# A hybrid decoder layer on one core: sums of the FFN's hidden tiles spread over K blocks, a pool opened with waits per tile, the last products reordered

## The chip, the cores and the metric

The kernel runs on one core of a Trainium2 chip. The metric is the device time of one execution, in microseconds (us); lower is better. In this text PE is the matrix engine (TensorE), PEld its weight load, DVE the vector engine, ACT the scalar engine, POOL is GpSimd and SP the engine that issues most loads. ACT issues DMAs as well, and such an issue stands in the same in-order queue as ACT's arithmetic (ACTq in the rows).

## The reference, cut to what matters

One decoder layer on 512 tokens of width 2048, all in fp32: a norm, one input projection, four token mixers side by side, an output projection, then the feed-forward part, and a final norm.

```python
h = rmsnorm(x, norm_ffn_g[l])
x = x + swiglu(h, w_gate[l], w_up[l], w_down[l])   # (silu(h @ w_gate) * (h @ w_up)) @ w_down
...
return rmsnorm(x, norm_final_g)                    # D_FF = 5632, D_MODEL = 2048
```

The change touches the feed-forward part (FFN) and the final norm. Its hidden values, silu(gate) times up, are called h below.

## The kernel before

**Precision.** Every fp32 operand is split into a high part (ACT copies it, rounding to the short fp32r format) and a low part (DVE subtracts the high part from the operand): `split2`, lines 1043 and 1044. A product is three matmuls: high by high, low by high, high by low. So every weight tile costs ACT one copy and DVE one subtraction before PE can use it. `wh`/`wl` are the two halves of a weight step of the gate and up projection, `dh`/`dl` those of the down projection; three buffers hold high parts and four hold low parts, so the high part of step k+2 can't be written before PE has read that of step k-1.

**Seven products.** Gate and up projection, and the down projection, are each done as a 2x2 block product with seven block products (Strassen-Winograd), P1, P5, P6, P3, P7, P4, P2 in that order. Some of them need sums of weight tiles (`T`, formed on DVE, line 1123) and sums of h tiles (S1 to S4, `hs`, DVE).

**The FFN loop.** There are 11 groups `gi` of 512 hidden columns. A group is 28 steps: seven products by four steps `jj`. A step is two K blocks, a K block six matmuls (two token tiles by three). `strassen(k)` calls `w_ahead(k)`, which issues loads for later steps, forms the sum for step k+3 and splits the weights of step k+2; then after each K block it yields, and `run` gives every generator in `side` one hop (`step_side`, line 922). There is no scheduler: each engine works in the order in which the program was written.

**The side work.** After a group's P4 and again after its P2, `got_product` gates the result (`gated`: Silu on ACT, one multiply on DVE, for each of two token tiles) and appends `turn_h`, a generator that waits four hops, then does two halves with a hop between: four PE transposes (`ph`), and `h_sums`, which forms the S tiles, splits those that the down projection will want split, and writes ten tiles per group to DRAM (`ad`) by DMAs issued on ACT (`put`). All of a half's arithmetic and puts are written in one hop. P4's side work (token half 1) runs in P2; P2's (token half 0) runs in P1 of the next group.

**Down projection.** List `ds` holds the products of one K tile each: P1 and P5 alternating, P6 and P3, then P7 followed by P4 with P2's products in between. A product is 12 matmuls. `d_ahead` loads and splits two products ahead. Before the first product the FFN's pool `fp` (`sums`) is closed and the pool `dn` opened over its memory, with tiles for raw weights (`rw`), h tiles (`ar`, split `ah`/`al`), sums `T` and results `c`. In the P7, P4 stage every P7 and P4 forms a sum T on DVE, ACT copies its high part, DVE subtracts; a P2 needs only the two splits.

**Tail.** The last three products (`NT`) are done per token tile t and column half c. `V` holds P2's accumulators (token half 0), `U` those of P4 (token half 1). Squares of finished values go to `ssq`; `finish_tok` takes the square root, the reciprocal, scales four pieces of a token tile and stores them.

Of the kernel before, what the change touches and what calls it, by code (L numbers as in the profile page):

```python
# [39 lines left out]
def hybrid_kernel(ctx, tc, xT, wi, wt, wo, wgu, wdn, vec, rows, sgw, w2a2, g2, pbias, cmask, oneh, addc, fing, out):  # L40
# [14 lines left out]
    def t2(name, shape=(128, 512), dt=F32):  # L55
        return p2.tile(list(shape), dt, name=name, tag="s2")
# [954 lines left out]


    sums = ctx.enter_context(ExitStack())
    fp = sums.enter_context(tc.tile_pool(name="fp", bufs=4))
    xd = dpool.tile([KT, 128, S], F32, name="xd")
    PI = dict(P1=0, P5=1, P6=2, P3=3, P7=4, P4=6, P2=8)
    ad = dpool.tile([10, NG // 4, 128, 2, 256], F32, name="ad")
# [146 lines left out]

    part = {}

    def turn_h(gi, th, h):

        for _ in range(4):
            yield  # L1170
        for b in range(2):
# [5 lines left out]
            h_sums(gi, th, b, p)  # L1177
            yield

    held = {}  # L1180

    def h_sums(gi, th, b, ph):

        def put(p, t, u=0):
            nc.scalar.dma_start(ad[PI[p] + u, gi], t.rearrange("p (b t) -> p b t", b=2))

        def parts(p, src):
            hi, lo = t2("sh", dt=F32R), t2("sl", dt=F32R)
            split2(hi, src, lo)
            put(p, hi.bitcast(F32))  # L1190
            put(p, lo.bitcast(F32), 1)
        if (th, b) == (1, 0):
            held["A21"] = t2("hT")
            ac.activation(held["A21"], ph, AF.Copy)
        elif (th, b) == (1, 1):
            s1 = held["S1"] = t2("hs")
            parts("P4", ph)
            dv.tensor_add(s1, ph, held["A21"])
            put("P5", s1)
        elif (th, b) == (0, 0):  # L1200
            a11, s2 = t2("hT"), t2("hs")
            ac.activation(a11, ph, AF.Copy)
            put("P1", a11)
            dv.tensor_sub(s2, held.pop("S1"), a11)
            held["S2"] = s2
            put("P6", s2)
            s3 = t2("hs")
            dv.tensor_sub(s3, a11, held.pop("A21"))
            parts("P7", s3)
        else:  # L1210
            s4 = t2("hs")
            dv.tensor_sub(s4, ph, held.pop("S2"))
            put("P3", s4)
            parts("P2", ph)

    def got_product(gi, p, t, acc):

        def keep(name):
            part[name, t] = t2(name)
            ac.activation(part[name, t], acc, AF.Copy)  # L1220

        def gated(g, pre, u, i):
            ac.activation(g, pre, AF.Silu, scale=norm2.r[:, i:i + 1])
            dv.scalar_tensor_tensor(g, u, norm2.r[:, i:i + 1], g, op0=OP.mult, op1=OP.mult)
        if p == "P1":
            keep("c11")
        elif p == "P5":
            keep("c22")
        elif p == "P6":
            keep("c12")  # L1230
        elif p == "P3":
            dv.tensor_add(part["c12", t], acc, part["c12", t])
        elif p == "P7":
            dv.tensor_add(part["c22", t], acc, part["c22", t])  # L1234
        elif p == "P4":
            c = part["c21", t] = t2("c21")
            gated(c, acc, part.pop(("c22", t)), 2 + t)
            if t:
                side.append(turn_h(gi, 1, [part.pop(("c21", 0)), part.pop(("c21", 1))]))
        else:  # L1240
            c = part["c11", t]
            dv.tensor_add(c, acc, c)
            gated(c, c, part.pop(("c12", t)), t)
            if t:
                side.append(turn_h(gi, 0, [part.pop(("c11", 0)), part.pop(("c11", 1))]))

    bank = {}

# [57 lines left out]
    n2 = 0  # L1306
    for i, x in enumerate(rest):
        ds.append(x)
        if i % 2 and i > 2 or i == len(rest) - 4:
            ds.append(("P2", n2))  # L1310
            n2 += 1
    assert n2 == NK
# [59 lines left out]
    held.clear()  # L1372
    sums.close()
    mid.close()
    dn = ctx.enter_context(tc.tile_pool(name="dn", bufs=1))
    tags = dict(c=(512, 16), sqd=(512, 1), xq=(1024, 2), T=(1024, NK), ahl=(512, 8), rw=(1024, 5), ar=(512, 4))

    def dt(name, tag, dt=F32):
# [79 lines left out]
    def each():  # L1458
        return [(t, c) for t in range(2) for c in range(2)]
# [8 lines left out]
    def finish_tok(th, t, bank):  # L1468

        q = ssq[:, 2 * th + t]  # L1470
        r = t1("s2", (128, 4))
# [3 lines left out]
        dv.reciprocal(r[:, 3:4], r[:, 2:3])  # L1475
        tok = slice((2 * th + t) * 128, (2 * th + t + 1) * 128)
        for c in range(2):
            o = cf.pop((th, 1, t, c))
            ac.activation(o, o, AF.Copy, scale=r[:, 3:4])
            nc.scalar.dma_start(out[tok, 1024 + c * 512:1536 + c * 512], o)  # L1480
        for c in range(2):
            o = cf.pop((th, 0, t, c))
            dv.scalar_tensor_tensor(o, bank[c] if bank else o, r[:, 3:4], gain[0][:, c * 512:(c + 1) * 512], op0=OP.mult, op1=OP.mult)
            nc.sync.dma_start(out[tok, c * 512:c * 512 + 512], o)

    gain = []
    later = []
    for i in range(2, len(ds) - NT):
        p, kk = ds[i]
        d_ahead(i)  # L1490
        if ds[i] == ("P5", 0):
            V = banks(px)
            xq = load_xq(0, 1)
        elif ds[i] == ("P3", 6):
            turn_x(xq, V)
            xq = load_xq(1, 1)
        elif ds[i] == ("P7", 1):
            V = banks(px)
            turn_x(xq, V, True)
            xq = load_xq(0, 0)  # L1500
            for t, c in each():
                dv.tensor_add(cf[1, 1, t, c], V[t][c], cf[1, 1, t, c])
            V = banks(px)
        elif ds[i] == ("P4", 2):
            turn_x(xq, V)
            xq = load_xq(1, 0)
        elif ds[i] == ("P4", 12):
            turn_x(xq, U)
            del xq
        product(i)  # L1510
        del cutd[i]
        if kk % 2 or i == ends[p]:
            Ac.pop((p, kk // 2), None)
        if i == ends["P1"]:
            for t, c in each():
                cf[0, 0, t, c] = dt("c", "c")
                ac.activation(cf[0, 0, t, c], U[t][c], AF.Copy)
        elif i == ends["P5"]:
            for t, c in each():
                cf[1, 1, t, c] = dt("c", "c")  # L1520
# [22 lines left out]

    tail = range(len(ds) - NT, len(ds))
    d_ahead(len(ds) - NT)
    for th, bank in ((0, V), (1, U)):
        for t in range(2):
            for c in range(2):
                for i in tail:
                    if (ds[i][0] == "P4") == bool(th):  # L1550
                        product(i, [(t, c)])
                o = bank[t][c]
                if th:
                    cf[1, 0, t, c] = dt("c", "c")
                    square(1, 0, t, c, o)
                else:
                    dv.tensor_add(cf[0, 0, t, c], o, cf[0, 0, t, c])
                    square(0, 0, t, c, cf[0, 0, t, c])
            finish_tok(th, t, bank[t] if th else None)


def _constants():
# [81 lines left out]
```

## Time and profile before

| | us |
|---|---|
| median of three runs | 2352.35 (2351.2 to 2355.08) |
| the profiled execution, its own time | 2354.43 |
| its span in the trace | 2352.7 |
| granted PE clock, mean | 0.985 of full |
| mixers and output projection, to | 924 |
| FFN: gate and up projection, from 924 to | 1867 |
| down projection and final norm | to 2352.7 |

The trace is of the profiled execution: times in it run from the span's start. Its own time is 1.7 us more than its span and 2.08 us above the median. Bracketed at the end of a timeline row stands how long the engine was idle before the instruction and what released it.

### The profile page before, as it was taken

To read this page: it belongs to the slowest core of one execution; us is meant where nothing else is said; L and a number is where in the kernel's file an instruction comes from. 1 tells how busy PE (TensorE), PEld (TensorE's weight loads), DVE (VectorE), ACT (ScalarE), POOL (GpSimd) and SP (SyncE) were. 2 spreads that over 40 slices of the span, in tenths; PEclk is the share of its full clock that TensorE was granted. 3 is DMA by queue.
4 is the path that set the end of the run, shared out by engine and by line. 5 is a ranking of instruction groups with operands and counts; after the bars stand their busy time and mean duration, and the time that the engine had idled before them with its cause. 6 is when DMAs were issued, how large, how long until landed. Compare 5 with 4: busy or idle time off the path is not lost.

```text
span 2352.7 us, 29300 instructions
## 1 busy us (share of the span) xinstructions
PE 2245.9 (95%) x11064; PEld 1793.7 (76%) x11064; DVE 1567.0 (67%) x2341; ACT 1013.7 (43%) x1556; POOL 2.3 (0%) x16
## 2 busy tenths in 40 slices
PE   8999999999999997899999999999999879999996
PEld 6788878877777785678777777877877768888785
DVE  6555456654444447877867877777787667777775
ACT  5522222244444435544444444444445344543334
POOL 0000000000000000000000000000000000000000
PEclk9999999999999999999999999999999989999998
DMA  5232323232233235343444455354355187547884
GB/s 185 84 95 73 101 76 92 61 99 82 71 99 108 90 109 178 118 164 121 166 161 152 149 169 180 114 189 166 117 170 192 52 289 250 175 130 241 284 299 177
DMA packets 164541, 342.78 MB, mean 146 GB/s; under 512 B 29296, under 2 KB 34928, under 8 KB 164400
## 3 DMA queue, kind: packets, MB, share of 16 engines
q1 hardware_dynamic: 134832, 290.25, 38.6%
q10 hardware_dynamic: 29568, 50.66, 6.0%
q8 instruction: 87, 1.43, 0.3%
q14 instruction: 54, 0.44, 0.1%
HBM read 302.79 MB, written 38.05 MB: 145 GB/s over the span
## 4 chain that ended last, share of the span: by engine, by line
PE 73%; DVE 13%; ACT 7%; issue 4%; DMA 1%; ACTq 1%; SPq 0%; DVEq 0%
PE prod L1266 8%; PE prod L1267 8%; PE prod L1265 8%; PE acc L144 7%; PE acc L146 7%; PE acc L145 7%; PE bk L1340 4%; PE bk L1341 4%; PE bk L1339 4%; DVE wl L1044 3%; PE acc L162 3%; PE acc L164 2%; PE acc L163 2%; ACT wh L1043 2%; DVE dl L1044 2%
## 5 line engine op out<-in xcount | busy, mean ns | idle before, releaser
L1044 DVE TENSOR_TENSOR wl<-wq,wh 128x512 fp32r<-128x512 f32 x352 | 227.2, 687 | 116.2 <-ACT wh L1043 115.2
L1266 PE MATMUL prod<-wl,h 128*128 128x512 f32 x704 | 282.1, 401 | 22.3 <-DVE wl L1044 22.2
L1265 PE MATMUL prod<-wh,h 128*128 128x512 f32 x704 | 281.5, 400 | 16.4 <-ACT wh L1043 16.4
L1267 PE MATMUL prod<-wh,l 128*128 128x512 f32 x704 | 279.3, 397 | 0.0
L1043 ACT ACTIVATE wh<-wq 128x512 fp32r<-128x512 f32 x352 | 201.4, 623 | 176.0 <-PE prod L1267 105.5
L1339 PE MATMUL bk<-dh,ah 128*128 128x512 f32 x608 | 238.7, 393 | 19.2 <-ACT dh L1043 19.2
L106 DVE TENSOR_TENSOR wlo<-wraw,whi 128x1024 fp32r<-128x1024 f32 x127 | 155.3, 1223 | 140.1 <-ACT whi L105 139.8
L1340 PE MATMUL bk<-dl,ah 128*128 128x512 f32 x608 | 240.0, 395 | 3.7 <-DVE dl L1044 3.7
L1341 PE MATMUL bk<-dh,al 128*128 128x512 f32 x608 | 237.9, 391 | 0.0
L105 ACT ACTIVATE whi<-wraw 128x1024 fp32r<-128x1024 f32 x127 | 134.0, 1055 | 210.7 <-PE acc L145 105.4
L144 PE MATMUL acc<-xhi,whi 128*128 128x512 f32 x512 | 209.3, 409 | 5.6 <-ACT whi L120 5.2
L1043 ACT ACTIVATE wh<-T 128x1024 fp32r<-128x1024 f32 x132 | 139.8, 1059 | 156.9 <-PE prod L1267 111.5
L146 PE MATMUL acc<-xhi,wlo 128*128 128x512 f32 x512 | 200.8, 392 | 1.1 <-DVE wlo L106 1.1
L145 PE MATMUL acc<-xlo,whi 128*128 128x512 f32 x512 | 200.6, 392 | 0.4 <-DVE xlo L235 0.3
L1044 DVE TENSOR_TENSOR wl<-T,wh 128x1024 fp32r<-128x1024 f32 x132 | 161.4, 1223 | 38.3 <-ACT wh L1043 37.7
L1266 PEld LDWEIGHTS prod<-wl,h 128*128 128x128 f32 x704 | 135.3, 192 | 58.9 <-DVE wl L1044 30.9
L1265 PEld LDWEIGHTS prod<-wh,h 128*128 128x128 f32 x704 | 135.1, 192 | 53.7 <-ACT wh L1043 25.5
L1267 PEld LDWEIGHTS prod<-wh,l 128*128 128x128 f32 x704 | 135.2, 192 | 27.7
L1339 PEld LDWEIGHTS bk<-dh,ah 128*128 128x128 f32 x608 | 115.0, 189 | 44.5 <-issue 17.4
L1265 PE MATMUL prod<-wh,hb 128*128 128x512 f32 x352 | 139.7, 397 | 6.7 <-DVE c L1234 6.7
L1043 ACT ACTIVATE dh<-T 128x1024 fp32r<-128x1024 f32 x66 | 70.0, 1061 | 174.1 <-DVE T L1418 57.2
L1340 PEld LDWEIGHTS bk<-dl,ah 128*128 128x128 f32 x608 | 115.0, 189 | 32.3 <-DVE dl L1044 9.2
(316 smaller groups left out, 4159.5 us busy)
## 6 DMA issues: line engine op xcount, KB each, us to landing
wq<-in_wgu_dram SPq DMA_DIRECT2D x440, 256.0 KB, 3.6
rw<-in_wdn_dram SPq DMA_DIRECT2D x134, 512.0 KB, 4.8
wraw<-in_wi_dram SPq DMA_DIRECT2D x63, 512.0 KB, 3.7
wraw<-in_wt_dram SPq DMA_DIRECT2D x32, 512.0 KB, 3.6
wraw<-in_wo_dram SPq DMA_DIRECT2D x32, 512.0 KB, 3.6
ar<-ad SPq DMA_DIRECT2D x44, 256.0 KB, 4.1
ad<-sh ACTq DMA_DIRECT2D x33, 256.0 KB, 3.9
ad<-sl ACTq DMA_DIRECT2D x33, 256.0 KB, 4.1
```

What stands on the lines that cost most here:

```text
L106: dv.tensor_sub(lo, r, hi.bitcast(F32))
L144: pe.matmul(acc[b], wh, xh, start=(c == 0 and k == 0), stop=False)
L145: pe.matmul(acc[b], wh, xl, start=False, stop=False)
L146: pe.matmul(acc[b], wl, xh, start=False, stop=(c == nchunk - 1 and k == 3))
L1043: ac.activation(hi, src, AF.Copy)
L1044: dv.tensor_sub(lo, src, hi.bitcast(F32))
L1265: pe.matmul(acc[t], ah[:, tt], hi[:, u], start=first, stop=False, skip_group_check=more)
L1266: pe.matmul(acc[t], ah[:, tt], lo[:, u], start=False, stop=False, skip_group_check=more)
L1267: pe.matmul(acc[t], al[:, tt], hi[:, u], start=False, stop=(j == 7), skip_group_check=more)
L1339: pe.matmul(o, ah[:, a], hi[:, cc], start=fresh, stop=False, skip_group_check=True)
L1340: pe.matmul(o, ah[:, a], lo[:, cc], start=False, stop=False, skip_group_check=True)
L1341: pe.matmul(o, al[:, a], hi[:, cc], start=False, stop=last, skip_group_check=True)
```

## The change

In the FFN, `turn_h` and `h_sums` become one generator that does one or two operations per hop; the gating moves into it (P4's multiply, and for P2 Silu and multiply); each put is written a hop after what it stores. The pools `fp` and `dn` are opened with `reuse_waits="tile"`. In `ds` P2's products are spread so that the last stands four P4 products before the end. The tail finishes token half 0 earlier, in two pieces, ahead of the last P4 products, and scales and stores with other engines and queues.

```diff
-    fp = sums.enter_context(tc.tile_pool(name="fp", bufs=4))
+    fp = sums.enter_context(tc.tile_pool(name="fp", bufs=4, reuse_waits="tile"))
...
+    def turn_h(gi, th, h, us):
+
+        def put(p, t, u=0):
+            nc.scalar.dma_start(ad[PI[p] + u, gi], t.rearrange("p (b t) -> p b t", b=2))
...
+        rn = [norm2.r[:, 2 * th + t:2 * th + t + 1] for t in range(2)]
+        if th == 0:
+            yield
+            for t in range(2):
+                ac.activation(h[t], h[t], AF.Silu, scale=rn[t])
+        yield
+        for t in range(2):
+            dv.scalar_tensor_tensor(h[t], us[t], rn[t], h[t], op0=OP.mult, op1=OP.mult)
+        us.clear()
+        yield
+        yield
+        p = turned(0)
+        a = t2("hT")
+        ac.activation(a, p, AF.Copy)
+        if th:
...
+            return
+        put("P1", a)
+        yield
+        s2, s3 = t2("hs"), t2("hs")
+        dv.tensor_sub(s3, a, held.pop("A21"))
+        yield
+        hi = high("P7", s3)
+        dv.tensor_sub(s2, held.pop("S1"), a)
+        yield
+        put("P6", s2)
+        lo = low(s3, hi)
+        yield
+        put("P7", lo.bitcast(F32), 1)
+        p = turned(1)
+        hi = high("P2", p)
+        yield
+        s4 = t2("hs")
+        dv.tensor_sub(s4, p, s2)
+        yield
+        put("P3", s4)
+        lo = low(p, hi)
+        yield
+        put("P2", lo.bitcast(F32), 1)
...
-        if i % 2 and i > 2 or i == len(rest) - 4:
+        while n2 < NK and i >= 3 + n2 * 36 // (NK - 1):
             ds.append(("P2", n2))
             n2 += 1
...
-    dn = ctx.enter_context(tc.tile_pool(name="dn", bufs=1))
+    dn = ctx.enter_context(tc.tile_pool(name="dn", bufs=1, reuse_waits="tile"))
...
+        for dh, c in ((1, 0), (0, 0), (0, 1), (1, 1)):
+            o = cf.pop((th, dh, t, c))
+            if dh == 0:
+                dv.scalar_tensor_tensor(o, bank[c] if bank else o, r, gain[0][:, c * 512:(c + 1) * 512], op0=OP.mult, op1=OP.mult)
+            elif c:
+                dv.tensor_scalar(o, o, r, None, op0=OP.mult)
+            else:
+                ac.activation(o, o, AF.Copy, scale=r)
+            col = dh * 1024 + c * 512
+            (nc.sync if dh + c < 2 else nc.scalar).dma_start(out[tok, col:col + 512], o)
...
+        elif p == "P2" and i == ends["P2"]:
+            for t, c in each():
+                dv.tensor_add(cf[0, 0, t, c], V[t][c], cf[0, 0, t, c])
+                square(0, 0, t, c, cf[0, 0, t, c])
+            norm_tok(0, 0)
+            store_tok(0, 0, None)
+        elif p == "P4" and kk == NK - 1 - NT:
+            norm_tok(0, 1)
+            store_tok(0, 1, None)
...
+    for t in range(2):
+        for c in range(2):
+            for i in tail:
+                product(i, [(t, c)])
+            cf[1, 0, t, c] = dt("c", "c")
+            square(1, 0, t, c, U[t][c])
+        norm_tok(1, t)
+        if t == 0:
+            store_tok(1, t, U[t])
+    store_tok(1, 1, U[1])
```

**Where instructions stand.** ACT's queue in P1 of a group, before: from the first transposed half of P2's result (`hT`) on. `sh` is the high part of an h sum, `hs` the sum, `sl` its low part; `wh<-T` is the high part of a P5 step, in order the steps jj 0 and jj 1.

```order
L1202 ACTIVATE hT<-ph 128x512
L1185 DMA ad<-hT 128x512
L1185 DMA ad<-hs 128x512
L1043 ACTIVATE sh<-hs 128x512
L1185 DMA ad<-sh 128x512
L1185 DMA ad<-sl 128x512
L1043 ACTIVATE wh<-T 128x1024
L1185 DMA ad<-hs 128x512
L1043 ACTIVATE sh<-ph 128x512
L1185 DMA ad<-sh 128x512
L1185 DMA ad<-sl 128x512
L1043 ACTIVATE wh<-T 128x1024
```

The same place in the changed kernel; `wh<-T` are P5's steps jj 0 and 1 (2 follows behind these rows), `c` the copies of P1's result.

```order
L1205 ACTIVATE hT<-ph 128x512
L1172 DMA ad<-hT 128x512
L1043 ACTIVATE wh<-T 128x1024
L1176 ACTIVATE sh<-hs 128x512
L1172 DMA ad<-sh 128x512
L1043 ACTIVATE wh<-T 128x1024
L1172 DMA ad<-hs 128x512
L1249 ACTIVATE c_11232<-prod 128x512
L1249 ACTIVATE c_11237<-prod 128x512
L1172 DMA ad<-sl 128x512
L1176 ACTIVATE sh<-ph 128x512
L1172 DMA ad<-sh 128x512
```

Before, four puts and an h split stood ahead of P5's first high part, and three puts and a split between the first and the second. Now one put stands ahead of the first, a split and a put ahead of the second, and the rest behind it, between P5's steps; the put of a sum or a low part stands behind other work than before.

SP's queue where the FFN's last loads end and `dn`'s first loads begin, before, with the semaphores that each waits for (the DMAHW ones are eight lanes that all DMAs take in turn).

```order
L1354 DMA ar<-ad 128x512 [waits DMAHW7_49]
L1389 DMA rw<-in_wdn_dram 128x1024 [waits DMAHW4_49,DMAHW3_49,DMAHW5_49,DMAHW2_49,DMAHW6_49,DMAHW1_49,DMAHW7_49,DMAHW0_49,DVE_49]
L1389 DMA rw<-in_wdn_dram 128x1024
L1405 DMA ar<-ad 128x512
L1389 DMA rw<-in_wdn_dram 128x1024 x3
```

The same place in the changed kernel.

```order
L1377 DMA ar<-ad 128x512 [waits DMAHW7_49]
L1412 DMA rw<-in_wdn_dram 128x1024 [waits DMAHW2_49,DVE_49,PE_49]
L1412 DMA rw<-in_wdn_dram 128x1024 [waits DMAHW3_49]
L1428 DMA ar<-ad 128x512 [waits DMAHW4_49]
L1412 DMA rw<-in_wdn_dram 128x1024 [waits DMAHW5_49,DVE_49]
L1412 DMA rw<-in_wdn_dram 128x1024 [waits DMAHW7_49,DMAHW6_49,PE_49]
```

Before, the first load into `dn` waited for all eight DMA lanes, and so for every put of the last group. Now it waits for one lane, one count of DVE and one of PE, and the loads behind it for a lane or two each.

DVE's queue at the end of the program, before: from the sum T of P4 20 on (the products of a kind are numbered 0 to 21). `dl<-rw` is P2's last low part; `c<-bk,c` adds P2's accumulators, and the small rows are a token tile's norm.

```order
L1429 TENSOR_TENSOR T<-rw,T 128x1024
L1044 TENSOR_TENSOR dl<-T,dh 128x1024
L1429 TENSOR_TENSOR T<-rw,T 128x1024
L1044 TENSOR_TENSOR dl<-T,dh 128x1024
L1044 TENSOR_TENSOR dl<-rw,dh 128x1024
L1557 TENSOR_TENSOR c<-bk,c 128x512 x2
L1472 TENSOR_TENSOR s_18605<-ssq 128x2
L1473 TENSOR_TENSOR s_18605<-s_18605 128x1
L1475 RECIPROCAL s_18605<-s_18605 128x1
L1483 SCALAR_TENSOR_TENSOR c<-c,s_18605,gain 128x512 x2
L1557 TENSOR_TENSOR c<-bk,c 128x512 x2
```

The same place in the changed kernel, from the T of P4 19 on.

```order
L1452 TENSOR_TENSOR T<-rw,T 128x1024
L1044 TENSOR_TENSOR dl<-T,dh 128x1024
L1570 TENSOR_TENSOR c<-bk,c 128x512 x4
L1496 TENSOR_TENSOR s_18583<-ssq 128x2
L1497 TENSOR_TENSOR s_18583<-s_18583 128x1
L1499 RECIPROCAL s_18583<-s_18583 128x1
L1508 SCALAR_TENSOR_TENSOR c<-c,s_18583,gain 128x512 x2
L1510 TENSOR_SCALAR c<-c,s_18583 128x512
L1452 TENSOR_TENSOR T<-rw,T 128x1024
L1044 TENSOR_TENSOR dl<-T,dh 128x1024
L1496 TENSOR_TENSOR s_18613<-ssq 128x2
L1497 TENSOR_TENSOR s_18613<-s_18613 128x1
```

The additions of P2's accumulators and two token tiles' norm and scaling, which stood behind every T and dl, now stand ahead of the T of P4 20, and the second of them ahead of the T of P4 21.

## Rows read from the trace of the kernel before

**Rows 1.** The page's head: span; busy time of engines (share of the span) and instructions.

```profile
span 2352.7 us, 29300 instructions
...
PE 2245.9 (95%) x11064; PEld 1793.7 (76%) x11064; DVE 1567.0 (67%) x2341; ACT 1013.7 (43%) x1556; POOL 2.3 (0%) x16
```

**Rows 2.** Windows (us; busy PE, PEld, DVE, ACT, POOL; PEclk): three periods; one of six; sum.

```profile
sum 249.11, PE 238.48 PEld 193.23 DVE 194.04 ACT 118.74 POOL 0.00; mean PE 79.49 PEld 64.41 DVE 64.68 ACT 39.58 POOL 0.00
...
1121.81:1206.56 84.75, 81.08 (x352) 65.58 (x352) 64.87 (x94) 39.62 (x59) 0.00 (x0) 0.98 0.47 156
...
sum 508.22, PE 486.62 PEld 393.33 DVE 389.20 ACT 237.73 POOL 0.00; mean PE 81.10 PEld 65.56 DVE 64.87 ACT 39.62 POOL 0.00
```

**Rows 3.** Timeline of PE, end of P1 and start of P5 (start, duration, instruction, idle before).

```profile
1035.60 0.39 PE L1265 MATMUL prod<-wh,a 128*128 128x512 f32 x1
...
1038.11 0.39 PE L1267 MATMUL prod<-wh,a 128*128 128x512 f32 x1
1038.93 0.50 PE L1265 MATMUL prod<-wh,h 128*128 128x512 f32 x1 [0.44 <-ACT wh L1043]
1040.19 0.50 PE L1266 MATMUL prod<-wl,h 128*128 128x512 f32 x1 [0.76 <-DVE wl L1044]
...
1043.98 0.49 PE L1265 MATMUL prod<-wh,h 128*128 128x512 f32 x1 [1.00 <-ACT wh L1043]
1045.24 0.50 PE L1266 MATMUL prod<-wl,h 128*128 128x512 f32 x1 [0.77 <-DVE wl L1044]
```

**Rows 4.** Timeline of ACT, same place.

```profile
1036.06 0.63 ACT L1043 ACTIVATE sh<-hs 128x512 fp32r<-128x512 f32 x1 [2.88 <-DVE hs L1208]
...
1037.82 1.06 ACT L1043 ACTIVATE wh<-T 128x1024 fp32r<-128x1024 f32 x1 [1.13 <-DVE sl L1044]
...
1041.14 0.60 ACT L1043 ACTIVATE sh<-ph 128x512 fp32r<-128x512 f32 x1 [2.26 <-DVE hs L1212]
```

**Rows 5.** Timeline of DVE, from the gating of P2's result to P5's first split.

```profile
1028.31 0.75 DVE L1224 SCALAR_TENSOR_TENSOR c<-c,rn,c 128x512 f32<-128x512 f32 x1 [0.79 <-ACT c L1223]
...
1031.12 1.29 DVE L1044 TENSOR_TENSOR wl<-wq,wh 128x512 fp32r<-128x512 f32 x2
...
1037.33 1.29 DVE L1123 TENSOR_TENSOR T<-wq 128x512 f32<-128x512 f32 x2
1038.91 1.22 DVE L1044 TENSOR_TENSOR wl<-T,wh 128x1024 fp32r<-128x1024 f32 x1 [0.29 <-ACT wh L1043]
```

**Rows 6.** Timeline of all engines, end of FFN and start of down.

```profile
1876.99 1.03 PE L1175 MATMUL ph<-cm,c 128*128 128x128 f32 x8
...
1883.30 0.33 ACTq L1185 DMA_DIRECT2D ad<-sl  x1
1885.44 0.81 SPq L1389 DMA_DIRECT2D rw<-in_wdn_dram  x2
...
1891.96 0.69 DVE L1044 TENSOR_TENSOR al<-ar,ah 128x512 fp32r<-128x512 f32 x1 [8.70 <-DMA rw<-in_wdn_dram]
...
1894.98 0.77 PE L1339 MATMUL bk<-dh,ah 128*128 128x512 f32 x1 [16.95 <-ACT dh L1043]
```

**Rows 7.** Timeline of DVE in the P7/P4 stage of down.

```profile
2161.50 1.23 DVE L1044 TENSOR_TENSOR dl<-rw,dh 128x1024 fp32r<-128x1024 f32 x1 [1.21 <-ACT dh L1043]
2162.64 1.22 DVE L1426 TENSOR_TENSOR rw<-T,rw 128x1024 f32<-128x1024 f32 x1
2165.07 2.36 DVE L1044 TENSOR_TENSOR dl<-rw,dh 128x1024 fp32r<-128x1024 f32 x2 [1.21 <-ACT dh L1043]
```

**Rows 8.** Timeline of ACT in the tail.

```profile
2330.86 1.28 ACT L1474 ACT_TABLE_LOAD   x1
2332.16 0.30 ACT L1474 ACTIVATE s<-s,eps 128x1 f32<-128x1 f32 x1
...
2348.68 0.34 ACTq L1480 DMA_DIRECT2D out_dram<-c  x1
```

**Rows 9.** Window of the tail, from the last five products (60 matmuls) on; columns as before.

```profile
2318.62:2352.70 34.08, 15.86 (x61) 12.12 (x59) 15.87 (x29) 17.03 (x32) 0.00 (x0) 0.77 0.33 124
```

More of the change, by code (lines that the diff above doesn't have):

```diff
@@ L1165, in hybrid_kernel, with high, low, turned @@
     part = {}
[L1167 to L1171, printed above, removed]
+    held = {}
+    def turn_h(gi, th, h, us):
+        def put(p, t, u=0):
+            nc.scalar.dma_start(ad[PI[p] + u, gi], t.rearrange("p (b t) -> p b t", b=2))
+        def high(p, src):
+            hi = t2("sh", dt=F32R)
+            ac.activation(hi, src, AF.Copy)
+            put(p, hi.bitcast(F32))
+            return hi
+        def low(src, hi):
+            lo = t2("sl", dt=F32R)
+            dv.tensor_sub(lo, src, hi.bitcast(F32))
+            return lo
+        def turned(b):
             p = px("ph")
@@ L1176, in turn_h @@
                                  h[t][:, (2 * b + fb) * 128:(2 * b + fb + 1) * 128], ident)
-            h_sums(gi, th, b, p)
+            return p
+        rn = [norm2.r[:, 2 * th + t:2 * th + t + 1] for t in range(2)]
+        if th == 0:
             yield
[L1180 to L1195, printed above, removed]
+            for t in range(2):
+                ac.activation(h[t], h[t], AF.Silu, scale=rn[t])
@@ L1196, in h_sums @@
+        yield
[12 more added lines that the diff above has]
+            p = turned(1)
+            hi = high("P4", p)
+            yield
             s1 = held["S1"] = t2("hs")
-            parts("P4", ph)
-            dv.tensor_add(s1, ph, held["A21"])
+            dv.tensor_add(s1, p, a)
+            held["A21"] = a
+            yield
@@ L1199, in h_sums @@
             put("P5", s1)
[L1200 to L1214, printed above, removed]
+            lo = low(p, hi)
@@ new lines, in turn_h @@
+            yield
+            put("P4", lo.bitcast(F32), 1)
+            return
[6 more added lines that the diff above has]
+        dv.tensor_sub(s2, held.pop("S1"), a)
+        yield
+        put("P6", s2)
+        lo = low(s3, hi)
+        yield
+        put("P7", lo.bitcast(F32), 1)
+        p = turned(1)
+        hi = high("P2", p)
+        yield
+        s4 = t2("hs")
@@ L1216, in got_product @@
+        dv.tensor_sub(s4, p, s2)
+        yield
+        put("P3", s4)
+        lo = low(p, hi)
+        yield
+        put("P2", lo.bitcast(F32), 1)
     def got_product(gi, p, t, acc):
@@ L1220, in keep @@
             ac.activation(part[name, t], acc, AF.Copy)
-        def gated(g, pre, u, i):
-            ac.activation(g, pre, AF.Silu, scale=norm2.r[:, i:i + 1])
-            dv.scalar_tensor_tensor(g, u, norm2.r[:, i:i + 1], g, op0=OP.mult, op1=OP.mult)
         if p == "P1":
@@ L1235, in got_product @@
         elif p == "P4":
-            c = part["c21", t] = t2("c21")
-            gated(c, acc, part.pop(("c22", t)), 2 + t)
+            part["c21", t] = t2("c21")
+            ac.activation(part["c21", t], acc, AF.Silu, scale=norm2.r[:, 2 + t:3 + t])
             if t:
-                side.append(turn_h(gi, 1, [part.pop(("c21", 0)), part.pop(("c21", 1))]))
+                side.append(turn_h(gi, 1, *([part.pop((n, u)) for u in range(2)] for n in ("c21", "c22"))))
         else:
-            c = part["c11", t]
-            dv.tensor_add(c, acc, c)
-            gated(c, c, part.pop(("c12", t)), t)
+            dv.tensor_add(part["c11", t], acc, part["c11", t])
             if t:
-                side.append(turn_h(gi, 0, [part.pop(("c11", 0)), part.pop(("c11", 1))]))
+                side.append(turn_h(gi, 0, *([part.pop((n, u)) for u in range(2)] for n in ("c11", "c12"))))
     bank = {}
@@ L1308, in hybrid_kernel @@
         ds.append(x)
-        if i % 2 and i > 2 or i == len(rest) - 4:
+        while n2 < NK and i >= 3 + n2 * 36 // (NK - 1):
             ds.append(("P2", n2))
             n2 += 1
-    assert n2 == NK
     QUAD = dict(P1=(0, 0), P5=(0, 1), P6=(1, 1), P7=(0, 0), P2=(1, 0), P4=(1, 0))
@@ L1466, in square, with norm_tok @@
         ac.activation(dt("sqd", "sqd"), src, AF.Square, accum_out=ssq[:, 2 * th + t, col:col + 1])
-    def finish_tok(th, t, bank):
+    rn4 = {}
+    def norm_tok(th, t):
         q = ssq[:, 2 * th + t]
-        r = t1("s2", (128, 4))
+        r = rn4[th, t] = t1("s2", (128, 4))
         dv.tensor_add(r[:, 0:2], q[:, 0:2], q[:, 2:4])
@@ L1475, in finish_tok, with store_tok @@
         dv.reciprocal(r[:, 3:4], r[:, 2:3])
+    def store_tok(th, t, bank):
+        r = rn4[th, t][:, 3:4]
         tok = slice((2 * th + t) * 128, (2 * th + t + 1) * 128)
[L1477 to L1484, printed above, removed]
+        for dh, c in ((1, 0), (0, 0), (0, 1), (1, 1)):
[8 more added lines that the diff above has]
+            (nc.sync if dh + c < 2 else nc.scalar).dma_start(out[tok, col:col + 512], o)
     gain = []
@@ L1545, in hybrid_kernel @@
     d_ahead(len(ds) - NT)
[L1546 to L1559, printed above, removed]
+    for t in range(2):
[8 more added lines that the diff above has]
+    store_tok(1, 1, U[1])
 def _constants():
```

## The prediction

> **What bounds the kernel now.** I read the page's head first: PE is busy for 2245.9 of 2352.7 us [rows 1], so outside a few places the kernel is as long as its matmuls, and the change, which leaves their number as it is, can only give back what PE loses while it waits. Next the windows of the FFN's group periods, which should all be alike. They are not: three periods with a granted clock of 1.00 take 249.11 us together (83.04 each), six with 0.98 take 508.22 (84.70) [rows 2]. Then PE's timeline where P1 ends and P5 begins. Matmuls start every 0.227 us (eleven intervals from 1035.60 to 1038.11). From 1038.11 to 1045.24 there are 14 intervals, worth 3.18 us; they took 7.13. So 3.95 us are lost once per group, in four stalls, before P5's first and second step; the rows name ACT's `wh` and DVE's `wl` [rows 3]. With smaller ones I take 4.05.
>
> Why are those late? In ACT's timeline its queue waits 2.88 us for the sum `hs`, 1.13 for a low part `sl` ahead of the first `wh`, and 2.26 for the next `hs` [rows 4]. ACT is 40% busy (39.62 of 84.75 us [rows 2]); it is a ping-pong between two in-order queues. DVE, meanwhile, does the gating of the group's results and the splits that it must do anyway [rows 5]. The 0.98 periods are 1.66 us longer than the others with the same stalls: a stretch at the lower of PE's two levels (1.2 GHz) after the stall in six of nine.
>
> Two more places carry waits. At the end of the FFN, PE does its eight transposes at 1876.99, ACT issues the last put at 1883.30, SP's first load into `dn` goes at 1885.44, DVE can split at 1891.96, PE restarts at 1894.98, 16.95 us idle [rows 6]. And in the tail, 34.08 us from where 60 matmuls are left, with PE busy for 15.86 [rows 9].
>
> **The change, part by part.** *Spread sums, FFN.* The same instructions in other places; PE, DVE and ACT do the same work. I walk the queues by hand with the rows' durations, from the end of P2's last matmul (time 0). Behind each other, DVE's instructions start 1.14 to 1.20 us apart for 1024 columns [rows 7], 0.60 for 512 (two in 1.29 [rows 5]), 0.67 for a gate (0.75 long [rows 5]). P5's first matmul is due at four steps of 12 x 0.227 = 2.72 and eight transposes (1.03 [rows 6], about 0.9 as pitch): 11.8. DVE from -0.85 on, without a gap: `wl` of P1's second step, S1, two adds of P2's result, low part of P4 (done 2.75), `wl` (3.95), two gates (5.3), T (6.45), `wl` (7.7), T (8.85), `wl` of P5's first step (10.0). That is due at 12.0: the first stall pair is gone. Then S3, S2 and T, to 12.4. ACT: high of S3 at 10.7, its put (0.33), `wh` of P5's second step from 11.7 to 12.75, so `wl` to 14.0, due 14.7: the second pair is gone as well. Behind it two puts and a split of h: a put waits for the low part that DVE ends at 14.6, the high part of P2 follows to 15.6, its put to 16.0, `wh` of the third step to 17.05, `wl` to 18.3, due 17.43: 0.9 late. S4, a low part and a T are now ahead of the fourth `wl`, 21.85, due 21.05 after the first delay: 0.8 late. After that DVE needs 2.4 us per step of 2.72 and recovers. So 1.7 us remain of 4.05; bounds are 0 (each of the two has but 0.9 us to gain) and 3 (both stalls of the size of a `wl`, 1.2, and one more half). Ten boundaries: 10 x (4.05 - 1.7) = 23.5 us.
>
> *The clock.* A stall of 0.9 and one of 0.8, a step apart, are less than half of what three periods passed at 1.00 [rows 2, 3]; I take the drops as gone: 6 x 1.66 = 10.0 us. Bounds: all stay (0), all gone (10). With the stalls: -33.5.
>
> *`dn` opened with waits per tile.* Before, the load at 1885.44 waits for all lanes, that is, for the last put's landing: 2.14 us after its issue and 8.45 after the transposes began [rows 6]. Now it waits for a lane used long before, and for a count of DVE and one of PE. These counts can be no later than the second half's transposes and the sums of h behind them. If it is the transposes, the load leaves 8.45 us earlier than before; if it is DVE's last sum or low part, some 4. The 6.5 us from load to split and 3.0 to PE stay as they are. Behind the load on SP are only the other loads of `dn`; nothing else waits. I take -7, between -4 and -10 (the larger with less time at the lower clock level after a shorter gap).
>
> *P2 spread.* In the P7, P4 stage DVE's chain T, high part on ACT, low part takes 3.57 us per product (2161.50 to 2165.07), and a P2 in between another 1.14 [rows 7]. Two such and a P2: 8.28 us, against 3 x 2.72 = 8.16 on PE, so before this chain set the pace, by a little. With P2 spread by 36/21, 12 of the former go with 7 of the latter: 12 x 3.57 + 7 x 1.14 = 50.8 against 19 x 2.72 = 51.7. PE sets the pace: -2, less than 0.12 for each of some 20 such triples (bounds 0 and -3, with the stalls that such a lag makes).
>
> *The tail.* This part costs, I think. The additions of P2's accumulators, squares, norm and scaling now stand in DVE's queue ahead of the T of P4 20, and PE has little left to do meanwhile. From the start of P2 21 (60 matmuls left, as in the window of before): the low part of P4 19 ends at 3.25, four adds at 5.7; the last square ends at 6.6 on ACT; the table load takes 1.28, the root 0.30 [rows 8], the reciprocal and scaling bring DVE to 10.3; T of P4 20 to 11.5, its high part 12.55, low part 13.8; the next norm and scaling 16.55; T of P4 21 17.7, high part 18.8, low part 20.05. PE has 27 matmuls (P2 21, P4 18 and three of P4 19: 6.1 us), waits from 6.1 to 12.6 for the first of P4 20 and again to 18.8 for P4 21's. Then 27 more take 6.1 from about 20, and about 2 more at the lower clock: 28.4. From there a root, a scaling and the last put take about 3.7 as before, the put's landing 4.0 (2348.68 to the end [rows 1, 8]): 36.2 to 36.5, against 34.08 [rows 9]: +2.5, between -1 (clock at full level, loads of T earlier) and +4.
>
> The row of the table load begins at 2330.86 and the root's at 2332.16, right behind its end [rows 8]: nothing else is charged. The Trainium skill, "ScalarE: Activation LUTs", section "What ACT_TABLE_LOAD costs", gives about 1283 ns, which agrees with the row, and adds some 1380 ns of drain for each switch of set, which no row here shows. Since the load is now ahead of the last two splits, by that rule the end would come 1.4 us later; by the row it does not.
>
> **Sum**, on the profiled execution's 2354.43: -33.5 - 7 - 2 + 2.5 = -40.0, so 2314.4. That execution was 2.08 above the median of the runs shown: 2312 as a median.
>
> **Rivals.** *A: the boundary stall goes wholly.* My walk is 0.9 late twice; a slack of one instruction earlier (the low part before the put) would hide it. Then the FFN gains 40.5 + 10 = 50.5, 17 more: 2295. For it: ACT is 40% busy. Against it: a put still holds ACT's queue for DVE as in [rows 4], only elsewhere.
> *B: the clock still drops.* New stalls of 0.9 in a row, in the third and fourth step of P5, with a lower level behind them in six of ten groups: 10 more, 2322. For it: the size of the stall from which it drops is not shown in these rows.
> *C: the dn opening gains nothing*, because the loads behind it wait for the last puts' lanes anyway: the first that waits for two lanes is the fifth into `dn`. 7 more: 2319.
> *D: slower.* The four puts that now stand in P5's middle each hold ACT as long as the waits of before, 2.88, 1.13, 2.26 and 1.13 [rows 4], and all of it stalls PE: 7.4 us a group in place of 4.05, with the clock low in all ten: +33.5 + 6.6 in the FFN, with -6.5 of the rest 2386. From 4.7 us per group on, drops unchanged, the kernel is slower than before. Against it: ACT has 1.6 us to spare in each step of 2.72, and DVE's tiles are made a hop ahead of their puts.
> *E: the stalls only move*, 4.05 in P5's later steps and the clock as it was: -6.5 in all, 2346; without the dn gain too, 2353, no change.
>
> **How the numbers follow.** Forecast 0.45, A 0.17, B 0.18, C 0.08, D 0.06, E 0.06. The predicted time is the forecast's, 2312. The range must hold A, the forecast, B and C, and B with C (2329): 2291 to 2329, with 0.88 less what lies past their edges. This kernel's runs differ by 0.16% (2351.2 to 2355.08), so 0.2%, 4.7 us, is about what a measurement can tell. Faster by more than that: the forecast, A, B, C and half of E, 0.91; same, the other half with its like, 0.04; slower, D less its mild end, 0.05.
>
> **What would show it.** A period of about 80.5 us at PEclk 1.00 in place of 83 to 84.7; before P5's first and second step no idle time of PE, and before its third and fourth 0.4 to 0.9 us, released by `wl`. PE's idle before the down projection's first product 10 to 12 us instead of 16.95. In the tail PE idle twice for 5 to 6.5 us before the first matmuls of P4 20 and P4 21, released by `dh`, and a window of 36 us where it was 34.08. The prediction is wrong if ACT's puts in P5 wait over 2 us each (towards D), if no stall is left (A), or if some period still reads 0.98 (B); and on the tail, if P4 20's T is done before the norm.

## The result and the profile after

The changed kernel takes 2321.71 us (median of four runs, 2319.58 to 2322.39) against 2353.72 (four runs): ratio 0.9863, 95% interval 0.9846 to 0.988. That is inside the predicted range and on the forecast side; the forecast of 2312 was some 10 us too low. The profiled execution took 2322.26 us, its span is 2320.5.

First the FFN, windows of PE's periods (columns as in rows 2), one of nine and their sum:

```profile
1206.37:1287.22 80.85, 79.14 (x354) 64.39 (x353) 64.19 (x94) 39.85 (x59) 0.00 (x0) 1.00 0.50 165
...
sum 727.77, PE 712.35 PEld 579.34 DVE 577.57 ACT 358.67 POOL 0.00; mean PE 79.15 PEld 64.37 DVE 64.17 ACT 39.85 POOL 0.00
```

All nine read a clock of 1.00; their mean is 80.86 us, where the mean over [rows 2] is (249.11 + 508.22) / 9 = 84.15. PE's timeline in P5, where [rows 3] showed four stalls, has two idle rows left:

```profile
1045.70 0.50 PE L1290 MATMUL prod<-wl,h 128*128 128x512 f32 x1 [0.76 <-DVE wl L1044]
...
1049.24 0.50 PE L1290 MATMUL prod<-wl,h 128*128 128x512 f32 x1 [0.50 <-DVE wl L1044]
```

They stand at the third and fourth step of P5. From matmul start to matmul start these are 1.26 and 0.89 us where 0.227 is usual, so 1.03 and 0.67, together 1.70 us (so too at the other boundaries; one of ten, at 1125, loses 0.31 more). ACT's and DVE's timelines say why (ACT's rows first, then DVE's):

```profile
1041.88 0.35 ACTq L1172 DMA_DIRECT2D ad<-sl  x1
1042.33 0.60 ACT L1176 ACTIVATE sh<-ph 128x512 fp32r<-128x512 f32 x1 [1.37 <-DMA wq<-in_wgu_dram]
1042.96 0.33 ACTq L1172 DMA_DIRECT2D ad<-sh  x1
1043.33 1.06 ACT L1043 ACTIVATE wh<-T 128x1024 fp32r<-128x1024 f32 x1 [0.40 <-ACT sh L1176]
```

```profile
1041.16 0.69 DVE L1182 TENSOR_TENSOR sl<-hs,sh 128x512 fp32r<-128x512 f32 x1
1041.76 1.29 DVE L1123 TENSOR_TENSOR T<-wq 128x512 f32<-128x512 f32 x2
1044.42 1.23 DVE L1044 TENSOR_TENSOR wl<-T,wh 128x1024 fp32r<-128x1024 f32 x1 [1.37 <-ACT wh L1043]
```

The put of `sl` can't leave before DVE ends `sl` at 1041.85, and the high part of the third step, `wh`, stands behind it, a split of h and another put. DVE then waits 1.37 us for `wh`. (The page names a load as the releaser of `sh`; the put issued just before it is what ACT did there.)

Next the end of the FFN, all engines:

```profile
1840.56 0.33 ACTq L1172 DMA_DIRECT2D ad<-sl  x1
...
1842.65 6.20 SPq L1412 DMA_DIRECT2D rw<-in_wdn_dram  x2
...
1845.19 1.03 PE L1189 MATMUL ph<-cm,c 128*128 128x128 f32 x8
...
1846.45 0.33 ACTq L1172 DMA_DIRECT2D ad<-hT  x1
...
1847.84 0.33 ACTq L1172 DMA_DIRECT2D ad<-sh  x1
...
1850.00 0.33 SPq L1428 DMA_DIRECT2D ar<-ad  x1
...
1851.15 0.82 ACTq L1172 DMA_DIRECT2D ad<-sl  x1
...
1855.49 0.63 ACT L1043 ACTIVATE ah<-ar 128x512 fp32r<-128x512 f32 x1 [5.69 <-DMA ar<-ad]
...
1857.98 1.22 DVE L1441 TENSOR_TENSOR T<-rw 128x1024 f32<-128x1024 f32 x1 [1.13 <-DMA ad<-sl]
...
1860.34 0.79 PE L1362 MATMUL bk<-dh,ah 128*128 128x512 f32 x1 [14.12 <-ACT dh L1043]
```

The first load into `dn` now leaves 2.5 us before the transposes (in [rows 6], 8.45 behind them). But the merged row "x2" lasts 6.20 us: the second load waits until about 1848.5, 2.1 us after the put of `hT`, and the load of h until 1850.00, 2.2 us after the put of `sh`. SP's waits in this stretch (us in total, times, longest) name both puts:

```profile
SPq L1412 <- DMA ad<-hT: 5.5, 1, 5.5
...
SPq L1428 <- DMA ad<-sh: 1.1, 1, 1.1
```

PE is idle for 14.12 us instead of 16.95.

Last the tail, DVE's and then PE's timeline:

```profile
2285.61 1.23 DVE L1044 TENSOR_TENSOR dl<-T,dh 128x1024 fp32r<-128x1024 f32 x1 [1.21 <-ACT dh L1043]
2286.75 2.48 DVE L1570 TENSOR_TENSOR c<-bk,c 128x512 f32<-128x512 f32 x4
...
2294.01 1.22 DVE L1452 TENSOR_TENSOR T<-rw,T 128x1024 f32<-128x1024 f32 x1
...
2300.19 1.22 DVE L1452 TENSOR_TENSOR T<-rw,T 128x1024 f32<-128x1024 f32 x1
```

```profile
2296.43 0.79 PE L1362 MATMUL bk<-dh,ah 128*128 128x512 f32 x1 [8.79 <-ACT dh L1043]
...
2302.61 0.79 PE L1362 MATMUL bk<-dh,ah 128*128 128x512 f32 x1 [3.69 <-ACT dh L1043]
```

PE waits 8.79 and 3.69 us for P4 20 and 21, whose T stand behind the additions and the norms. The window from the last 60 matmuls on, which answers to [rows 9]:

```profile
2281.34:2320.54 39.20, 17.50 (x61) 12.35 (x59) 19.69 (x35) 14.83 (x29) 0.00 (x0) 0.74 0.29 108
```

Four starts of matmuls cut each trace into stages: the FFN's first and last product, the down projection's first product in `dn` (its row names `ah`), and the 60th matmul from the end. In us:

| kernel | FFN products | last to first in dn | to the last 60 | tail | median |
|---|---|---|---|---|---|
| before | 942.53 | 28.52 | 423.64 | 34.09 | 2353.72 |
| changed | 911.23 | 24.84 | 420.99 | 39.20 | 2321.71 |
| e1 spread only | 911.24 | 26.09 | 423.22 | 33.01 | 2320.30 |
| e2 all but spread | 941.89 | 23.66 | 420.86 | 39.01 | 2352.90 |
| e3 gate in place | 927.75 | 25.63 | 420.43 | 38.84 | 2341.28 |
| e4 old tail | 911.14 | 23.13 | 423.32 | 33.01 | 2316.00 |
| e5 gate moved only | 922.25 | 20.75 | 419.84 | 40.40 | 2330.25 |
| e6 half later | 897.66 | 24.63 | 421.63 | 39.12 | 2309.16 |
| e7 norms after sums | 911.02 | 23.15 | 420.13 | 36.12 | 2317.43 |
| e8 pool order | 912.84 | 23.46 | 420.11 | 39.96 | 2322.44 (one run) |
| e9 hop, old tail, tags | 896.66 | 22.23 | 426.50 | 33.01 | 2303.86 |
| e10 hop, new tail, tags | 898.19 | 22.00 | 420.33 | 32.89 | 2299.21 |

The stages are of one profiled execution each, and that need not be the median one: it took 0.7 us more than the median before, 2.1 less in e2 and 3.0 less in e3. Where two kernels share the code of a stage, it repeats within about two microseconds, except for e9's third stage.

At the opening (24.84 and 23.13 for the same code) most of the spread lies ahead of the transposes, in the granted clock. Windows over the last matmuls there, in the changed kernel and in e4:

```profile
1839.60:1842.80 3.20, 3.20 (x8) 2.52 (x9) 2.04 (x4) 1.33 (x2) 0.00 (x0) 0.50 0.44 163
```

```profile
1838.80:1842.80 4.00, 4.00 (x18) 3.33 (x19) 2.46 (x4) 1.34 (x2) 0.00 (x0) 1.00 0.35 131
```

Eight matmuls at the lower level (0.50), as also before, in e3, e6 and e8, take some 1.6 us more. So PE's idle time before `dn`'s first product says more about the pool than the stage does: 16.95 us before, 16.95 in e1, which has the old pool as well (the row below is e1's), 13.43 to 14.12 in the seven kernels with waits per tile and the old tags, and 12.70 to 13.06 in e8, e9 and e10, with another order of tags.

```profile
1861.47 0.77 PE L1363 MATMUL bk<-dh,ah 128*128 128x512 f32 x1 [16.95 <-ACT dh L1043]
```

### The profile page after: what moved, and what is told of

Same layout as the page of the kernel before. It is cut to its first block, busy times and chain, and to the rows that moved or that the text cites. A ratio compares the mean times of both kernels' runs of the same rounds, so it can differ in the third digit from the quotient of the medians.

```text
span 2320.5 us, 29307 instructions
## 1 busy us (share of the span) xinstructions
PE 2232.2 (96%) x11064; PEld 1787.1 (77%) x11064; DVE 1562.5 (67%) x2345; ACT 1013.7 (44%) x1552; POOL 2.3 (0%) x16
## 4 chain that ended last, share of the span: by engine, by line
PE 80%; DVE 10%; ACT 5%; DMA 2%; issue 2%; ACTq 1%; SPq 0%; DVEq 0%
PE prod L1290 9%; PE prod L1291 9%; PE prod L1289 9%; PE acc L144 7%; PE acc L146 7%; PE acc L145 7%; PE bk L1363 5%; PE bk L1364 5%; PE bk L1362 5%; PE acc L162 3%; PE acc L164 3%; PE acc L163 3%; DVE wl L1044 2%; DMA wq<-in_wgu_dram 1%; ACT wh L1043 1%
## 5 line engine op out<-in xcount | busy, mean ns | idle before, releaser
L1290 PE MATMUL prod<-wl,h 128*128 128x512 f32 x704 | 277.7, 394 | 20.3 <-DVE wl L1044 20.2
```

Of the source, the lines that this page charges most:

```text
L1290: pe.matmul(acc[t], ah[:, tt], lo[:, u], start=False, stop=False, skip_group_check=more)
```

## The experiments

**e1, the spread alone.** The kernel before, with `turn_h` and `got_product` of the changed one, and nothing else.

```diff
-    def turn_h(gi, th, h):
...
-    def h_sums(gi, th, b, ph):
...
+    def turn_h(gi, th, h, us):
...
```

> The kernel before with the new turn_h and its gating alone. Theory: the FFN's gain is all of the change's gain; ten periods of 80.85 us at clock 1.00 in place of 84.15, so about 31 us less than before, 2322 to 2323, the same as the changed kernel. Rival (part of the gain hangs on the pools or on the order of the down projection): 2330 or more, periods longer than 81.

2320.30 us, ratio 0.9866 (0.985 to 0.9883): all that the change gains, the FFN at 911.24. That is 1.7 us below the range expected, but the theory holds and the rival doesn't: the rest of the change together gains nothing. The FFN takes as long as in the changed kernel although `fp` is the old pool, so the waits per tile of `fp` bring nothing there.

**e2, all but the spread.** The old `turn_h`, `h_sums` and `gated` in the changed kernel.

```diff
+        if (th, b) == (1, 0):
+            held["A21"] = t2("hT")
...
+        def gated(g, pre, u, i):
```

> The changed kernel with the old turn_h and the old gating in got_product; the pool dn per tile, the P2 spread and the new tail stay. Theory: these three come to about zero together: -3.7 (opening), -2.7 (P7/P4 stage), +5.1 (tail), so 2352 to 2354 with group periods of 83 to 85 us. Rival (each gains, as each was put in): 2345 or less.

2352.90, ratio 0.9997 (0.9988 to 1.0006): no change. In the profiled executions the opening (-4.9) and the P7/P4 stage (-2.8) gain, and the tail gives 4.9 back. So the tail is a step that costs.

**e3, the gating in place.** Sums, splits and puts stay spread; Silu and multiply go back to where the product ends.

```diff
-            for t in range(2):
-                ac.activation(h[t], h[t], AF.Silu, scale=rn[t])
...
+            gated(part["c21", t], acc, part["c22", t], 2 + t)
...
+            gated(part["c11", t], part["c11", t], part["c12", t], t)
```

> The changed kernel with the gating done at once where the product ends, as before, and only the sums, splits and puts spread over hops. Theory (the stalls came from the ping-pong of sums and puts between ACT and DVE): DVE waits some 0.8 us twice for Silu at P1's start, which P5's first step has in hand (its low part was 2 us early); the period stays within 80.8 to 82, the time within 0 to 10 us of the changed kernel. Rival (it was the moved gating that freed DVE): periods of 83 or more, 20 us or more slower than the changed kernel.

2341.28, 19.6 us slower than the changed kernel by the medians; the profiled executions differ by 16.0, and the FFN by 16.5, 1.65 per boundary. Neither expectation holds: I had allowed 10 us and periods up to 82, the rival asked for 20 and 83, and the periods are 82.5. The rival is nearer. DVE's timeline at P2's end shows one of two waits for Silu, and PE's the price (in P1, and in P5's second and third step):

```profile
1113.46 0.75 DVE L1248 SCALAR_TENSOR_TENSOR c<-c,rn,c 128x512 f32<-128x512 f32 x1 [0.80 <-ACT c L1247]
```

```profile
1115.46 0.50 PE L1289 MATMUL prod<-wl,a 128*128 128x512 f32 x1 [0.32 <-DVE wl L1044]
...
1124.82 0.50 PE L1289 MATMUL prod<-wl,h 128*128 128x512 f32 x1 [0.37 <-DVE wl L1044]
...
1127.90 0.50 PE L1288 MATMUL prod<-wh,h 128*128 128x512 f32 x1 [0.30 <-ACT wh L1043]
1129.16 0.50 PE L1289 MATMUL prod<-wl,h 128*128 128x512 f32 x1 [0.76 <-DVE wl L1044]
```

Two waits of 0.8 are 1.6 us, and PE loses 1.65 a group. From 1114.13 to 1123.54 DVE's timeline has no idle row. So it has nothing in hand between P2's end and P5's steps, and the sizes fit: what it waits there comes out at PE.

**e4, the old order and tail.** `ds` and the last loop as before.

```diff
-        while n2 < NK and i >= 3 + n2 * 36 // (NK - 1):
+        if i % 2 and i > 2 or i == len(rest) - 4:
...
-            norm_tok(0, 0)
-            store_tok(0, 0, None)
...
+            finish_tok(th, t, bank[t] if th else None)
```

> The changed kernel with the old order of P2's products and the old tail. Theory: the tail gets its 5.1 us back (34 us from the last 60 matmuls to the end) and the P7/P4 stage loses its 2.7: some 2 to 3 us faster than the changed kernel, about 2319. Rival (the longer tail is the price of the per-tile pool or of the FFN's earlier end, not of the order): no change, 2321 to 2322, with the tail at 39.

2316.00 (three of four runs within 0.03 of it, one 2322.29), 5.7 us faster than the changed kernel: the tail is back at 33.01, 6.2 shorter where 5.1 had been expected, and the stage before it 2.3 longer, as the theory has it. The other 1.7 lie in the opening, which this kernel did not touch: there its profiled execution has no matmuls at the lower level.

**e5, the gating moved, the sums in bursts.**

```diff
-            p = turned(1)
-            hi = high("P4", p)
...
+        for b in range(2):
+            h_sums(gi, th, b, turned(b))
+            yield
```

> The changed kernel with the gating in hops, but the sums, splits and puts of a half in one burst again, as before. With the gating in place and the sums spread the period was 82.5 us, 1.65 longer than in the changed kernel. Theory A (the two parts add up: the gating costs DVE two idle waits of 0.79 us, the bursts the rest): periods of 81.4 to 82.5, the time 2327 to 2338. Theory B (the gating alone was the cause and the spread of the sums does nothing): 80.9 and 2322. Theory C (either alone gives little, since DVE then stalls on the other): 83.5 or more, 2345 or more.

2330.25: theory A. PE's timeline at P5's first steps has lost the first pair of [rows 3] and kept the second:

```profile
1126.25 0.49 PE L1285 MATMUL prod<-wh,h 128*128 128x512 f32 x1 [1.32 <-ACT wh L1043]
1127.51 0.50 PE L1286 MATMUL prod<-wl,h 128*128 128x512 f32 x1 [0.77 <-DVE wl L1044]
```

Against before, the gating alone takes 20.3 us out of the FFN (942.53 to 922.25), the spread of sums alone 14.8 (e3), both 31.3, where the sum would be 35.1: the two parts add up but for 4 us. The windows of two neighbouring periods show the clock as well:

```profile
1285.07:1368.07 83.00, 80.78 (x354) 65.52 (x352) 64.55 (x94) 39.62 (x59) 0.00 (x0) 0.98 0.47 157
1368.07:1449.43 81.36, 79.16 (x353) 64.39 (x352) 64.36 (x94) 39.62 (x59) 0.00 (x0) 1.00 0.48 159
```

**e6, the second half a hop later.** One line in the changed kernel:

```diff
         lo = low(s3, hi)
         yield
+        yield
         put("P7", lo.bitcast(F32), 1)
```

> The changed kernel with one more hop before the put of P7's low part and the second half of P2's result, so that the high part of P5's third step stands ahead of them on ACT. Theory (the two stalls left, 1.03 and 0.67 us in P5's third and fourth step, come from that put and that h split ahead of it): they go or shrink to under half; period 79.2 to 80.0, 2305 to 2313. Rival (DVE has no time in hand there and the stall moves to the next steps): period 80.6 to 81, 2320 to 2322.

2309.16, ratio 0.9806 (0.9791 to 0.9822), 12.5 us faster than the changed kernel. PE's timeline has no idle row left in P5's four steps and one in the step behind them, where 0.40 us are lost from start to start; the period is 79.35:

```profile
1051.85 0.50 PE L1291 MATMUL prod<-wl,h 128*128 128x512 f32 x1 [0.24 <-DVE wl L1044]
```

```profile
1119.18:1198.53 79.35, 78.69 (x353) 64.45 (x352) 64.17 (x94) 39.50 (x60) 0.00 (x0) 1.00 0.49 167
```

So the put and the split of h ahead of the third `wh` were the cause of both stalls; of their 1.70 us, 1.3 are gained and 0.40 moved on.

**e7, norms after the sums.** The changed kernel's early finish of token half 0 moved behind `d_ahead`:

```diff
     d_ahead(len(ds) - NT)
+    for t, c in each():
+        dv.tensor_add(cf[0, 0, t, c], V[t][c], cf[0, 0, t, c])
+        square(0, 0, t, c, cf[0, 0, t, c])
+    for t in range(2):
+        norm_tok(0, t)
+        store_tok(0, t, None)
```

> The changed kernel with P2's additions, squares, norms and stores of token half 0 put behind the sums and splits of the last three P4 products instead of ahead of them. Theory (the tail is 39.2 us long because T of P4 20 and 21 stand behind two norms on DVE): PE no longer waits 8.8 and 3.7 us; the norms now end later themselves, so the tail is about 35 and the time 2317 to 2318. Rival (P4's last steps wait for their loads or for buffers): PE still waits, tail 39, no change.

2317.43, as the theory has it, but partly by luck: the tail is 36.12, 3.1 shorter where 4.2 had been expected, and the opening, which this kernel did not touch, is 1.7 shorter. The mechanism is the theory's: PE's two long waits are now 1.55 and 1.57 us:

```profile
2286.83 0.50 PE L1362 MATMUL bk<-dh,ah 128*128 128x512 f32 x1 [1.55 <-ACT dh L1043]
...
2290.40 0.79 PE L1362 MATMUL bk<-dh,ah 128*128 128x512 f32 x1 [1.57 <-ACT dh L1043]
```

**e8, another order of dn's tags.**

```diff
-    tags = dict(c=(512, 16), sqd=(512, 1), xq=(1024, 2), T=(1024, NK), ahl=(512, 8), rw=(1024, 5), ar=(512, 4))
+    tags = dict(ahl=(512, 8), rw=(1024, 5), ar=(512, 4), T=(1024, NK), xq=(1024, 2), sqd=(512, 1), c=(512, 16))
```

> The changed kernel with dn's tags laid out in another order (ahl, rw, ar, T, xq, sqd, c), so that the first T isn't laid over the tile that the last put reads. Theory (what is left of the opening is SP's lanes: the second weight load and the h load wait until puts issued after the transposes have landed, and T waits for the last put by only 1.1 us more): from the last FFN matmul to the down projection's first product 23.7 us instead of 24.8, one time 2319 to 2322. Rival (the memory under the last put holds the opening): 20 us or less.

The opening is 23.46 us, 23.7 had been expected; in DVE's timeline the T follows the low part without a wait:

```profile
1857.66 0.69 DVE L1044 TENSOR_TENSOR al<-ar,ah 128x512 fp32r<-128x512 f32 x1 [4.84 <-ACT ah L1043]
1858.27 1.22 DVE L1441 TENSOR_TENSOR T<-rw 128x1024 f32<-128x1024 f32 x1
```

In the time (2322.44, one run) this can't be seen. But PE's idle time is 12.70 us instead of 14.12, and in e9 and e10, which have this edit too, 13.06 and 12.86 for the 13.87 of e6. So 0.8 to 1.4 us are due to the order of tags, and the rival's 20 us or less does not come.

**e9 and e10, the edits together.** e9 is e6, e4 and e8 in one. e10 is e6, e8 and a tail as in e7, with both norms ahead of both stores, and all stores issued on SP:

```diff
+    for t in range(2):
+        norm_tok(0, t)
+    for t in range(2):
+        store_tok(0, t, None)
...
-            (nc.sync if dh + c < 2 else nc.scalar).dma_start(out[tok, col:col + 512], o)
+            nc.sync.dma_start(out[tok, col:col + 512], o)
```

> The changed kernel with three of the edits tried one by one: one more hop before the second half of P2's result, the old order of P2's products with the old tail, and dn's tags in the other order. Theory (the three places are apart in time, so their gains add up): from the changed kernel -12.5 for the hop, -5.7 for the old tail, -1 for the tags: 2302 to 2304. Rival (a gain in the FFN is given back at the down projection's start, where the loads and the last puts meet): 2307 or more.

> The changed kernel with the hop, the other order of tags, and a tail that keeps the P2 spread: additions, norms and stores of token half 0 behind the last sums, both norms ahead of both stores, and every store issued on SP, so that no put stands in ACT's queue. Theory (with P4's sums free the tail is a chain of four norms and scalings on DVE and ACT, 4.63 us each; taking the two first norms together and the puts off ACT shortens it by some 4 us to 32): 2300 to 2302. Rival (the chain is bound by DVE's scaling alone, so the order of norms and the queue of the puts change nothing): tail 36, 2304 to 2306.

e9 takes 2303.86, as its theory has it, though its third stage, 426.50, is 3.2 longer than e4's with the same order: from 2183.8 to 2187.2 PE runs eight matmuls at a granted clock of 0.50, behind a wait that e4 has as well. e10 takes 2299.21, ratio 0.9769 (0.9755 to 0.9782), 0.8 below the range expected. Its tail is 32.89, so the P2 spread can be kept with a short tail. Why it is shorter than e7's, rows of ACT's timeline say (e7 first, then e10):

```profile
2306.75 0.60 ACT L1489 ACTIVATE sqd<-bk 128x512 f32<-128x512 f32 x1 [1.55 <-DVE c L1510]
```

```profile
2288.64 0.58 ACT L1490 ACTIVATE sqd<-bk 128x512 f32<-128x512 f32 x1
```

In e7 the squares of a token tile stand on ACT behind a put that waits for DVE's last scaling of the tile before; in e10 they follow at once, and the last two token tiles are 2.96 us apart (scaling to scaling, 2288.01 to 2290.97) instead of 4.63. e10 changed two things, the order of norms and stores and the queue of the stores; these rows speak for the queue, but no kernel separates the two. e10 beats both kernels: 22.5 us less than the changed one.

## Why the prediction was right, and where it was off

*Spread sums: right, place and size.* Forecast 1.7 us left of 4.05 per boundary, 0.9 in P5's third and 0.8 in its fourth step; measured 1.03 and 0.67 there. The periods came to 80.86 for 80.5. With the clock the term was -33.5; the FFN's products take 31.3 less. What the walk did not split is which edit does it: e3 and e5 show that moving the gating is the larger half. I had charged it only as two multiplies without a gap, and did not price DVE's idle 0.79 before each ([rows 5] has one). Rival A (the stall goes wholly) needed one more edit, e6, and even there 0.40 is left. One reading was wrong: 39.62 of 84.75 us are 47%, not 40% (43% is ACT's share of the span); no term of the sum uses it, only the argument for rival A.

*The clock: right.* 0.98 in none of nine periods. Rival B is out.

*P2 spread: right*, -2.65 for -2.

*`dn` opened per tile: direction right, under half the size.* The stage is 3.7 us shorter for -7, and PE's idle time, which is what the pool acts on, 2.8 (16.95 to 14.12). The step that failed is "now it waits for a lane used long before": that was true of the first load alone, and T needs two, with the load of h behind them. Each DMA takes the next of eight lanes and waits for the one before on it, and these were puts issued after the transposes. Rival C had named this wait, though from a later load on. That the lanes hold these loads is read from SP's waits and the times of the puts; no kernel was run with the puts on other lanes. e1, with the old pool, is idle as long as the kernel before, so the 2.8 are the pool's (3.5 at most, in e3), and the new `turn_h` brings nothing to them. The other 0.8 lie ahead of the transposes.

*The tail: right in kind, forecast at half its size*, +5.1 for +2.5. The mechanism was the one walked: two waits for `dh`. The walk's first line was off: "the low part of P4 19 ends at 3.25". It ended at 2286.84, 5.50 us after the last 60 matmuls began (2281.34), since DVE and ACT had fallen behind PE in the last P4 products; everything behind it moved by 2.3 (T of P4 20 ended at 13.9, forecast 11.5). I had set DVE level with PE there, although the P7, P4 chain is 3.57 us for PE's 2.72 and P2 gives way at the end. Against e4's old tail, 33.01, the cost is 6.2: the 34.09 of before hold one more stretch at the lower level (near 2326.7 to 2330.1) than e1's, e4's and e9's 33.01.

*The table load: no drain.* The Trainium skill, "ScalarE: Activation LUTs", section "What ACT_TABLE_LOAD costs", would have put 1.4 us more at the table load. Rows of the changed kernel's ACT timeline don't show it, the load starting 0.01 us behind the instruction before it and the root 0.02 us behind the load:

```profile
2290.46 1.28 ACT L1498 ACT_TABLE_LOAD   x1
2291.76 0.29 ACT L1498 ACTIVATE s<-s,eps 128x1 f32<-128x1 f32 x1
```

The sum: -31.3 - 3.7 - 2.65 + 5.1, and 0.35 from the FFN's later start, is -32.2, which is what the profiled executions differ by (2354.43 to 2322.26), where -40 had been forecast: 2 in the FFN, 3 at the opening and 3 in the tail are missing. The stages are those of single executions, so a microsecond or two of this at the opening and in the tail is chance.

## What to carry to other kernels

Where two in-order queues feed each other, write one operation of the side work per step, and each DMA issue behind the next step's own work; then walk both queues by hand against the step's due time, which here gave the remaining stalls to 0.2 us. Work that finishes early results goes behind the sums and splits that the matrix engine waits for next, not ahead of them, where PE has little left to do meanwhile. Before a difference of a microsecond or two between two traces is given to an edit, look at the granted clock of the stage. A pool that frees memory by tile still waits for DMA lanes: look at every load that the first product needs.

## What was not expected of the hardware

The last put's landing got longer once loads left early. Its issue to the load that waited for it was 2.14 us in [rows 6]; in the changed kernel it was issued at 1851.15 among loads of 512 KB, and T was released at 1857.98, 6.8 us later. The DMA views have the median of such puts, before (1875 to 1897) and in the changed kernel (1838 to 1862, one of the three issued before the loads left):

```profile
ad<-sl ACTq DMA_DIRECT2D x2, 256.0 KB, 2.1
```

```profile
ad<-sl ACTq DMA_DIRECT2D x3, 256.0 KB, 5.4
```

And the lower clock level (1.2 GHz, in the periods that read 0.98) came where much was lost in one place: in six of nine periods before, with 3.8 to 4.3 us lost in four stalls; in two of nine in e5, with 1.1 to 1.6 and 1.03 lost one after the other; in none of nine in the changed kernel, with 1.03 and 0.67 lost at rows 3.5 us apart; and in none of nine in e3, which loses 3.2 us per boundary, but at five places from P1 to P5's fourth step. So the sum of what is lost does not decide it. What does, these runs don't show: three periods before passed at 1.00 with the same four stalls, and seven in e5 with the same two.
